# Recurrent branch of a four-mixer network: head outputs on the two halves of PSUM, products with the identity taken out, gate and bonus in the transposed layout

## The chip, the cores and the metric

The kernel runs on one core of a Trainium2 chip. The metric is the device time of one execution in microseconds. Three runs of the kernel before gave 2129.01, 2131.92 and 2132.62 us; the median is 2131.92 us. One further execution was recorded by the hardware profiler; it is the one whose rows are read below.

## The reference, cut to what matters

A network of two layers works on 512 tokens of width 1024, all in float32. Each layer projects the tokens, runs four mixers side by side (a windowed attention, a recurrent branch, an attention with forget gates, an attention over the 256 or fewer best keys), merges their gated outputs, and ends in a feed-forward part (dense in layer 0, eight experts in layer 1). The change touches the recurrent branch alone, which has 4 heads of 64:

```python
def step(state, inp):
    r_t, w_t, k_t, v_t, kk_t, a_t = inp
    sa = jnp.einsum('bhvk,bhk->bhv', state, -kk_t)
    state = (state * w_t[:, :, None, :] + sa[..., None] * (kk_t * a_t)[:, :, None, :]
             + v_t[..., None] * k_t[:, :, None, :])
    return state, jnp.einsum('bhvk,bhk->bhv', state, r_t)
...
y = ((y - ym) * lax.rsqrt(yv + RWKV_GN_EPS)).reshape(B, S, RWKV_W) * gn_g + gn_b
bonus = (jnp.sum(r_h * k_h * r_k, axis=-1, keepdims=True) * v_h).reshape(B, S, RWKV_W)
return ((y + bonus) * g).astype(p.dtype)
```

## The kernel before, in words

**Large products.** Projections, merge and feed-forward split each float32 operand into a high and a low part and run three products (L111, L112, L113) of 128 by 128 weights with 512 moving columns. ScalarE makes the high part of a weight block (L98), VectorE the low part (L99).

**The recurrent branch** (`rwkv`, L761 to L970) works on 8 chunks of 64 tokens. The 4 heads are two groups `g` of two heads `par`; a group's two heads lie on partitions 0 to 63 and 64 to 127 of a tile. A plain float32 product is two instructions in the trace, so four products show as x8; a transposition by `nc.tensor.transpose` shows as one. The stages:

- *Preparation* (`rwkv_prep`, L650 to L719), once for each group: normalised keys, two products with `wa_up` for decay and rate (L678, L683), the scaled keys `KBt` and queries `ARt`, and the bonus factor, four products with two columns each (L716).
- For each half of the sequence (`c0` = 0 and 4, four chunks):
  - *Pair matrices* `AM` (L819): for each pair of chunks and each head four products of 64 rows by 128 columns; then transpositions (L829, L830).
  - *Inversion* of the 64 by 64 triangles: 16 by 16 blocks by way of DRAM (`invert16`), then two levels of products (L848).
  - *Gap products* (L875, L885, L886): for each chunk the matrices `G` and `AP`, with a copy `xak` by ScalarE (L879) in the middle and another (L891) at the end.
  - *Rounds*, one for each chunk: `sa` = G + AP S, where G is brought in by a product with the identity (L901) and four small products are added (L906); `VS` written from it (L909 on VectorE, L910 on ScalarE); the output `y`, for each head a product with the state (L917) and one with `VS` (L919), all on the half of PSUM that the chunk has; the next state `u` = S + K'V, again with an identity product (L923) and four small ones (L928), then scaled by VectorE (L933) and copied by ScalarE (L937).
  - After two rounds the *normalisation* of 128 tokens (L941 to L967): statistics, scale and offset, bonus, gate product (L961), two transpositions (L965), and the split into high and low part (`put_o`, L512 to L514).

**Order.** The program is traced once and a planner of the framework lays down every engine's order beforehand from priorities and estimated durations; on the chip each engine then works its list in that order, waiting where a semaphore is not yet set. The recurrent branch has the highest priority (`hot`), and the work around it (value projection, the three attentions, gates and merge) is put where the branch waits. The branch's output is merged last of the four (`merge`). PSUM has eight banks; tags `r` and `y` are one bank each, so every stage of the branch passes through one or two banks. SBUF tiles with the tag `rw` come from a pool of 26.

Of the kernel before, what the change touches and what calls it, by code (L numbers as in the profile page):

```python
# [9 lines left out]
F32 = mybir.dt.float32  # L10
# [8 lines left out]
P = 128  # L19
# [17 lines left out]
TAGS = dict(rw=26, qk=14, o=12, pt=7, v=4, x=8, lc=4)  # L37
# [19 lines left out]
class Net:  # L57
# [219 lines left out]
    def load_vecs(self, layer):  # L277
# [5 lines left out]
        for name, src in (("mu", I["rwkv_mu"][layer]), ("w0", I["rwkv_w0"][layer]), ("a0", I["rwkv_a0"][layer]),  # L283
                          ("k_k", I["rwkv_k_k"][layer]), ("k_a", I["rwkv_k_a"][layer]),
                          ("r_k", I["rwkv_r_k"][layer].rearrange("h d -> (h d)")),
                          ("gb", I["gate_bias"][layer].rearrange("i d -> (i d)"))):
# [18 lines left out]
        self.gn = self.vec.tile([P, 2, 256], F32, name="gn", tag="gn")  # L305
        nc.sync.dma_start(self.gn[:, 0], I["rwkv_gn_g"][layer:layer + 1, :].to_broadcast([P, 256]))
        nc.sync.dma_start(self.gn[:, 1], I["rwkv_gn_b"][layer:layer + 1, :].to_broadcast([P, 256]))
# [342 lines left out]
    def rwkv_prep(self, g, r, k, wa, th, bonus):  # L650
# [26 lines left out]
        ps = self.ps("r")  # L677
        nc.tensor.matmul(ps, self.wa_up[0:64, gs], th[0:64], start=True, stop=True)  # L678
# [3 lines left out]
        ps = self.ps("r")  # L682
        nc.tensor.matmul(ps, self.wa_up[64:128, gs], wa[64:128], start=True, stop=True)  # L683
        a = self.bt("rw")
        nc.scalar.activation(a, ps, AF.Tanh, scale=0.5, bias=self.vcol("a0", g, True))
# [19 lines left out]
        for q in range(2):  # L705
            for par in range(2):
# [7 lines left out]
        bps = self.ps("r")  # L714
        for tb in range(TB):
            nc.tensor.matmul(bps[:, tb * 2:tb * 2 + 2], r[:, tb * P:(tb + 1) * P], self.halves[:, 0:P:64], start=True,  # L716
                             stop=True)
        nc.vector.tensor_copy(bonus[:, :, g], bps[:, 0:8].rearrange("p (t e) -> p t e", t=TB))
        return kb, ar, pc  # L719
# [40 lines left out]
    def rwkv(self, layer, pr):  # L760
        nc, bp = self.nc, self.bp  # L761
        r, k, v, wa, gl = pr[0:2], pr[2:4], pr[4:6], pr[6], pr[7]
        r4 = "p (c a t) -> p c a t"
        bonus = bp.tile([P, TB, 2, 2], F32, name="bonus", tag="bonus")
        nc.scalar.activation(wa[0:64], wa[0:64], AF.Tanh)
        KBt, ARt, pc = [], [], []
        for g in range(2):
            kb, ar, p_ = self.rwkv_prep(g, r[g], k[g], wa, wa, bonus)
# [6 lines left out]
        vt = [self.bt("rw").rearrange("p (t c) -> p t c", t=2) for _ in range(2)]  # L775
# [9 lines left out]

        for tb in range(TB):
# [4 lines left out]
            nc.scalar.copy(vt[tb // 2][:, tb % 2], ps[:, 0:256])  # L791
            p4 = ps[:, 0:256].rearrange("p (g e d) -> p g e d", g=2, e=2)
            for half in range(2):
                src = slice(64 * half, 64 * half + 64)
                ch = 2 * tb + half
                nc.vector.tensor_copy(VS(0, ch)[64:128], p4[src, :, 0])
                nc.vector.tensor_copy(VS(1, ch)[0:64], p4[src, :, 1])
        S = bp.tile([P, 2, 64], F32, name="S", tag="S", bufs=2)
        nc.vector.memset(S, 0.0)
# [3 lines left out]
        SD = SDs[0]  # L803
        ho = [self.new_o(("rwkv", g), "rw") for g in range(2)]
        idb = self.ident64[:, None].to_broadcast([P, 8, 64])
        for c0 in (0, 4):
# [4 lines left out]
            for c1 in (c0, c0 + 2):  # L811
                am = []
                for par in range(2):
                    rows = slice(64 * par, 64 * par + 64)
                    ps = self.ps("r")
                    for j in range(2):
                        for g in range(2):
                            i = 2 * j + g
                            nc.tensor.matmul(ps[:, i * P:(i + 1) * P], KB_(g, c1 + j)[rows], AR_(g, c1 + j)[rows],  # L819
                                             start=True, stop=True)  # L820
                    a = self.bt("rw").rearrange("p (i t) -> p i t", i=4)
                    nc.vector.tensor_mul(a, ps.rearrange("p (i t) -> p i t", i=4),
# [19 lines left out]
            def each(fn):  # L842
                ps = self.ps("r")
                for i in range(8):
                    for par in range(2):
                        rows = slice(64 * par, 64 * par + 64)
                        a, b2 = fn(c0 + i // 2, i % 2, par, i, rows)
                        nc.tensor.matmul(ps[rows, i * 64:(i + 1) * 64], a, b2, start=True, stop=True)  # L848
                return ps.rearrange("p (i t) -> p i t", i=8)

            def lower(ch, g, par):
                return am_(ch, g, par)[64 * par:64 * par + 64, 64 * par:64 * par + 64]
# [4 lines left out]
            self.invert16(c0 // 4, AM, tt, tT)  # L857
            for l in range(4, 6):
# [10 lines left out]
            for ch in range(c0, c0 + 4):  # L869
                ps = self.ps("r")  # L870
                for g in range(2):
                    for par in range(2):
                        rows = slice(64 * par, 64 * par + 64)
                        orow = slice(64 - 64 * par, 128 - 64 * par)
                        nc.tensor.matmul(ps[rows, g * 64:(g + 1) * 64],  # L875
                                         am_(ch, g, par)[orow, 64 * par:64 * par + 64], VS(par, ch)[orow, g],
                                         start=True, stop=True)
                x = bp.tile([P, 2, 64], F32, name="xak", tag="xak", bufs=2)
                nc.scalar.copy(x, ps[:, 0:128].rearrange("p (g t) -> p g t", g=2))  # L879
# [973 lines left out]
```

## Time and profile before

| what | us |
|---|---|
| median of three runs | 2131.92 |
| the profiled execution, its own time | 2129.68 |
| its span in the trace | 2127.9 |
| TensorE (PE) busy | 2040.7 |
| PE weight loads (PEld) busy | 1590.5 |
| VectorE (DVE) busy | 1365.3 |
| ScalarE (ACT) busy | 918.8 |
| GpSimd (POOL) busy | 150.3 |

The recurrent branch runs from about 60 to 333 us in layer 0 and from about 1020 to 1302 us in layer 1, mixed with other work. The busy time of PE counts each product from its start to its modelled end, and the ends of consecutive products overlap; how much PE time a product takes is read from the distance between its start and the start of the next. In the timeline, instructions of one line that follow each other stand in one row with a count; the first column is the start, the second the length.

### The profile page before, as it was taken

The page shows a single profiled execution, that of the slowest core. Times are in us where ns is not written, and L with a number is a line of the kernel's source. Part 1 is how long each engine was busy: PE and PEld are TensorE (multiplying, and loading weights), DVE is VectorE, ACT ScalarE, POOL GpSimd, SP SyncE. Part 2 cuts the span into 40 slices and gives each one's busy share as a digit, 9 for nine tenths or more (in the row PEclk, how much of TensorE's full clock was granted, in tenths as well). Part 3 has the DMA queues.
Part 4 walks back from the last instruction along what each step waited for, and adds up shares of the span by engine and source line. Part 5 has one row for each costly group of instructions (what it writes and reads, how often), then busy time and mean ns, then how long its engine had stood idle before and what let it go on. Part 6 is the DMA issues. An engine that isn't in the chain of part 4 may idle for free. (4 is left out here: it accounts for less than half of the span.)

```text
span 2127.9 us, 31168 instructions
## 1 busy us (share of the span) xinstructions
PE 2040.7 (96%) x11252; PEld 1590.5 (75%) x11252; DVE 1365.3 (64%) x2732; ACT 918.8 (43%) x1579; POOL 150.3 (7%) x211
## 2 busy tenths in 40 slices
PE   8999999999999999999999989999989999999984
PEld 7777767778888888888777767778877666677663
DVE  5775779844563333235686768844569777788778
ACT  3454533333232222113454533332317666677663
POOL 1020200000000000000011110000000000000034
PEclk9999999999999999999999999999999999999997
DMA  5231213243343334234221112323438988898872
GB/s 169 69 75 44 54 36 87 80 124 99 100 153 93 95 99 134 93 96 122 67 67 43 47 43 70 90 70 99 145 131 330 334 294 308 295 338 304 292 278 77
DMA packets 275537, 295.08 MB, mean 139 GB/s; under 512 B 23909, under 2 KB 203977, under 8 KB 275369
## 3 DMA queue, kind: packets, MB, share of 16 engines
q1 hardware_dynamic: 268296, 274.42, 40.4%
q0 software_dynamic: 7072, 18.49, 2.7%
q8 instruction: 97, 1.59, 0.3%
q14 instruction: 72, 0.58, 0.1%
HBM read 277.26 MB, written 15.60 MB: 138 GB/s over the span
## 5 line engine op out<-in xcount | busy, mean ns | idle before, releaser
L99 DVE TENSOR_TENSOR wlo<-wraw,whi 128x1024 fp32r<-128x1024 f32 (+1 forms) x218 | 265.4, 1218 | 373.4 <-ACT whi L98 370.4
L111 PE MATMUL ps_mm<-xh,whi 128*128 128x512 f32 (+1 forms) x1288 | 494.3, 384 | 3.2 <-ACT gate L977 2.6
L113 PE MATMUL ps_mm<-xh,wlo 128*128 128x512 f32 (+1 forms) x1288 | 494.3, 384 | 3.1 <-DVE rs L259 3.1
L98 ACT CAST whi<-wraw 128x1024 fp32r<-128x1024 f32 (+1 forms) x218 | 228.0, 1046 | 621.1 <-PE ps_mm L112 380.0
L112 PE MATMUL ps_mm<-xl,whi 128*128 128x512 f32 (+1 forms) x1288 | 495.1, 385 | 0.3 <-DVE xl L233 0.3
L111 PEld LDWEIGHTS ps_mm<-xh,whi 128*128 128x128 f32 x1288 | 243.9, 190 | 49.3 <-ACT gate L977 3.1
L113 PEld LDWEIGHTS ps_mm<-xh,wlo 128*128 128x128 f32 x1288 | 244.0, 190 | 47.4 <-DVE wlo L99 3.4
L112 PEld LDWEIGHTS ps_mm<-xl,whi 128*128 128x128 f32 x1288 | 244.0, 189 | 47.4 <-issue 4.8
L1152 DVE TENSOR_TENSOR wlo<-mwraw,whi 128x1024 fp32r<-128x1024 f32 (+1 forms) x98 | 124.1, 1281 | 18.9 <-ACT whi L1151 17.5
L1151 ACT CAST whi<-mwraw 128x1024 fp32r<-128x1024 f32 (+1 forms) x98 | 95.9, 1005 | 14.1 <-PE ps_t L1502 9.5
L472 ACT COPY bt_pt<-ps_t 128x512 f32<-128x512 f32 (+2 forms) x80 | 41.8, 522 | 100.2 <-PE ps_t L469 99.7
L1152 DVE TENSOR_TENSOR mwlo<-mwraw,mwhi 128x1024 fp32r<-128x1024 f32 (+1 forms) x62 | 71.8, 1174 | 7.0 <-ACT mwhi L1151 6.5
L453 ACT ACTIVATE bt_pt<-ps_s,mx 128x256 f32<-128x256 f32 (+3 forms) x128 | 62.0, 488 | 16.8 <-DVE mx L447 14.2
L444 DVE TENSOR_REDUCE mx<-ps_s 128x2 f32<-128x512 f32 (+3 forms) x80 | 48.5, 606 | 22.7 <-PE ps_s L408 22.0
L260 POOL TENSOR_TENSOR rs<-rs,mhalf 128x1 f32<-128x1 f32 x16 | 13.8, 861 | 693.7 <-DVE rs L259 693.7
L1151 ACT CAST mwhi<-mwraw 128x1024 fp32r<-128x1024 f32 (+1 forms) x62 | 61.0, 999 | 3.5 <-DMA mwraw<-in_exp_w_dram 2.3
L1113 DVE TENSOR_TENSOR bt_pt<-bt_pt,ps_mm 128x512 f32<-128x512 f32 x22 | 15.1, 687 | 70.5 <-PE ps_mm L113 63.1
L611 DVE MAX8 m<-bt_pt 128x8 f32<-128x256 f32 (+2 forms) x96 | 53.6, 558 | 2.2
L469 PE MATMUL ps_t<-ident,bt_pt 128*128 128x128 f32 x272 | 50.8, 282 | 4.2 <-DVE bt_pt L463 3.2
L1152 DVE TENSOR_TENSOR wlo<-ring,whi 128x1024 fp32r<-128x1024 f32 (+1 forms) x45 | 51.4, 1159 | 2.5 <-ACT whi L1151 1.5
L612 DVE MATCH_REPLACE8 bt_pt<-m,bt_pt 128x256 f32<-128x256 f32 (+2 forms) x96 | 52.0, 542 | 0.0
L111 PE MATMUL ps_mm<-bt_o,whi 128*128 128x512 f32 x128 | 51.2, 400 | 0.4 <-ACT gate L977 0.4
(709 smaller groups left out, 4172.0 us busy)
## 6 DMA issues: line engine op xcount, KB each, us to landing
mwraw<-in_exp_w_dram SPq DMA_DIRECT2D x124, 512.0 KB, 6.7
wraw<-in_w_in_dram SPq DMA_DIRECT2D x106, 512.0 KB, 3.7
wraw<-in_ffn_w_dram SPq DMA_DIRECT2D x66, 512.0 KB, 3.7
ring<-in_exp_w_dram SPq DMA_DIRECT2D x60, 512.0 KB, 6.0
wraw<-in_exp_w_dram SPq DMA_DIRECT2D x32, 512.0 KB, 6.0
mwraw<-in_exp_w_dram SPq DMA_DIRECT2D x36, 384.0 KB, 5.6
wraw<-in_w_branch_dram SPq DMA_DIRECT2D x20, 512.0 KB, 3.6
wraw<-in_w_out_dram SPq DMA_DIRECT2D x16, 512.0 KB, 3.7
```

The costliest lines, as they stand in the source:

```text
L98: nc.scalar.copy(h, src)
L99: (low or nc.vector).tensor_sub(l, src, h.bitcast(F32))
L111: mm(ps, wh, xh, start=start, stop=False)
L112: mm(ps, wh, xl, start=False, stop=False)
L113: mm(ps, wl, xh, start=False, stop=stop)
L444: nc.vector.tensor_reduce(mx[:, 0:nh], s3, op=OP.max, axis=AX.X)
L453: nc.scalar.activation(p3[:, h], s3[:, h], AF.Exp, bias=nm[:, h:h + 1], scale=0.125, accum_out=mx[:, 4 + h:5 + h])
L469: nc.tensor.transpose(pt[:, i * P:(i + 1) * P], p3[:, h, kb * P:(kb + 1) * P], self.ident)
L611: nc.vector.max(m8, sc[:, :nk])
L612: nc.vector.match_replace(sc[:, :nk], m8, sc[:, :nk], REPL)
L1151: self.chain("hi", lambda: nc.scalar.copy(hi[:, :n], src))
L1152: self.chain("lo", lambda: nc.vector.tensor_sub(lo[:, :n], src, hi[:, :n].bitcast(F32)))
```

## The change

What it does, stage by stage:

- The two `wa_up` products are issued one after the other into two banks (`r` and `y`).
- The bonus factor is one product with `halves` for all 512 tokens, at 128 by 512, and multiplied into `v`. Gate and offset are prepared once for each group in the layout with channels on partitions (`rwkv_gate`, after the first inversion), with the norm's scale and offset as per-partition columns. The broadcast copies `gn` go.
- The `AM` products of the two heads alternate, into the banks `r` and `y`.
- The gap products are made for two chunks at a time.
- In a round the identity products go: `G` is added by VectorE while `VS` is written, the old state is scaled ahead into `Sp` and added when the new state is read out of PSUM. The first round leaves out the products with the zero state.
- The outputs of a group's two heads go to the two halves of PSUM (chunk and group side by side), and are held behind the products of the next state by `issue_after`.
- After the normalisation eight products with a 64 by 64 identity bring the output into the transposed layout; it is multiplied by the gate and the prepared offset is added there.
- The pool `rw` has 28 tiles in place of 26, the scratch for dynamic DMA 4096 in place of 8192.

```diff
-        ps = self.ps("r")
-        nc.tensor.matmul(ps, self.wa_up[0:64, gs], th[0:64], start=True, stop=True)
+        ps, pa = self.ps("r"), self.ps("y")
+        nc.tensor.matmul(ps, self.wa_up[0:64, gs], wa[0:64], start=True, stop=True)
+        nc.tensor.matmul(pa, self.wa_up[64:128, gs], wa[64:128], start=True, stop=True)
...
+    def rwkv_gate(self, g, r, v, gl):
+        nc = self.nc
+        ps = self.ps("r")
+        nc.tensor.matmul(ps, self.halves, r, start=True, stop=True)
+        nc.vector.tensor_mul(v, v, ps)
+        ps = self.ps("r")
+        nc.tensor.matmul(ps, self.g_up[:, g * P:(g + 1) * P], gl, start=True, stop=True)
+        nc.scalar.activation(r, ps, AF.Copy, scale=self.vcol("gn_g", g))
+        nc.vector.scalar_tensor_tensor(v, v, self.vcol("gn_b", g), ps, op0=OP.add, op1=OP.mult)
+        return r, v
...
-                nc.vector.tensor_copy(VS(1, ch)[0:64], p4[src, :, 1])
+                nc.scalar.copy(VS(1, ch)[0:64], p4[src, :, 1])
...
+                pss = self.ps("r"), self.ps("y")
+                for j in range(2):
+                    for g, par in pairs:
+                        i = 2 * j + g
+                        rows = rows_[par]
+                        mm(pss[par][:, i * P:(i + 1) * P], KB_(g, c1 + j)[rows], AR_(g, c1 + j)[rows], start=True,
+                           stop=True)
...
-                    sa = self.ps("r")
-                    nc.tensor.matmul(sa[:, 0:128], self.ident, G[ch - c0].rearrange("p g t -> p (g t)"), start=True,
-                                     stop=True)
...
-                    nc.vector.tensor_copy(VS(0, ch)[0:64], s3[0:64])
-                    nc.scalar.copy(VS(1, ch)[64:128], s3[64:128])
+                        nc.vector.tensor_add(VS(0, ch)[0:64], s3[0:64], Gc[0:64])
+                        nc.vector.tensor_add(VS(1, ch)[64:128], s3[64:128], Gc[64:128])
...
+                            first = mm(u[rows_[par], g * 64:(g + 1) * 64], KT(ch)[:, g, rows_[par]], VS(par, ch)[:, g],
+                                       start=True, stop=True)
...
+                                nc.vector.scalar_tensor_tensor(Sn[:, g], us, d, Sp[:, g], op0=OP.mult, op1=OP.add)
...
+                            st.enter_context(self.tc.issue_after(first.ins))
                         for g in range(2):
+                            for par in (1, 0):
+                                o = yps[rows_[1 - par], half, g]
+                                if ch:
+                                    mm(o, ARt[g][ch // 4][:, ch % 4, 1 - par], SD[:, g, par], start=True, stop=False,
+                                       skip_group_check=True)
+                                mm(o, am_(ch, g, par)[:, rows_[1 - par]], VS(par, ch)[:, g], start=not ch, stop=True,
+                                   skip_group_check=True)
...
+                                nc.vector.tensor_scalar(Sp[:, g], S[:, g], pc[g][:, ch + 1:ch + 2], None, op0=OP.mult)
...
+                for half in range(2):
+                    for g, par in pairs:
+                        o = g * P + half * 64
+                        src = rows_[1 - par]
+                        mm(ps[rows_[par], o:o + 64], y[src, 2 * half + g], self.ident64[src], start=True, stop=True)
                 for g in range(2):
-                    self.put_o(ho[g], ts, ps[:, g * P:(g + 1) * P])
+                    gg, gb = go[g]
+                    t = bp.tile([P, P], F32, name="yt", tag="yt", bufs=2)
+                    nc.vector.tensor_mul(t, ps[:, g * P:(g + 1) * P], gg[:, ts])
+                    nc.vector.tensor_add(t, t, gb[:, ts])
+                    self.put_o(ho[g], ts, t)
```

## Rows read from the trace of the kernel before

**Rows 1.** The page, busy time, share of span, instructions.
```profile
PE 2040.7 (96%) x11252; PEld 1590.5 (75%) x11252; DVE 1365.3 (64%) x2732; ACT 918.8 (43%) x1579; POOL 150.3 (7%) x211
```

**Rows 2.** Windows: length, busy PE, PEld, DVE, ACT, POOL, granted clock, DMA share, GB/s.
```profile
60.00:333.00 273.00, 264.68 (x1947) 198.40 (x1946) 194.20 (x598) 132.38 (x338) 33.49 (x51) 0.99 0.22 55
1020.00:1302.00 282.00, 270.65 (x1965) 202.24 (x1965) 204.30 (x619) 135.09 (x340) 33.41 (x50) 0.99 0.20 52
```

**Rows 3.** Timeline of PE, large products back to back (start, length, line, tiles, form).
```profile
203.18 0.40 PE L111 MATMUL ps_mm<-xh,whi 128*128 128x512 f32 x1
203.41 0.39 PE L112 MATMUL ps_mm<-xl,whi 128*128 128x512 f32 x1
```

**Rows 4.** Timeline of PE, one round of the recurrence.
```profile
207.85 0.46 PE L901 MATMUL ps_r<-bt_rw,ident 128*128 128x128 f32 x2
208.23 0.45 PE L906 MATMUL ps_r<-S,bt_rw 64*64 64x64 f32 x8
208.61 0.50 PE L113 MATMUL ps_mm<-xh,wlo 128*128 128x512 f32 x1
208.95 0.40 PE L111 MATMUL ps_mm<-xh,whi 128*128 128x512 f32 x1
...
209.66 0.28 PE L917 MATMUL ps_y<-SD,bt_rw 128*64 128x64 f32 x2
209.78 0.28 PE L919 MATMUL ps_y<-bt_rw 128*64 128x64 f32 x2
...
210.46 0.49 PE L923 MATMUL ps_r<-S,ident 128*128 128x128 f32 x2
210.87 0.45 PE L928 MATMUL ps_r<-bt_rw 128*64 128x64 f32 x8
211.26 0.33 PE L469 MATMUL ps_t<-ident,bt_pt 128*128 128x128 f32 x1
```

**Rows 5.** Timeline of PE, gap products of one chunk.
```profile
180.03 0.45 PE L875 MATMUL ps_r<-bt_rw 64*64 64x64 f32 x8
180.41 0.33 PE L407 MATMUL ps_s<-bt_qk 128*128 128x128 f32 x1
...
180.91 0.34 PE L885 MATMUL ps_r<-xak,bt_rw 64*64 64x64 f32 x4
...
181.57 0.44 PE L469 MATMUL ps_t<-ident,bt_pt 128*128 128x128 f32 x2
```

**Rows 6.** Timeline of PE, pair matrices of one head and two chunks.
```profile
226.22 0.40 PE L111 MATMUL ps_mm<-xh,whi 128*128 128x512 f32 x1
226.54 1.16 PE L819 MATMUL ps_r<-bt_rw 64*128 64x128 f32 x8
227.63 0.39 PE L524 MATMUL ps_s<-m_swa,identb 128*128 128x512 bf16 x1
```

**Rows 7.** Timeline of PE, the first product with wa_up.
```profile
67.43 1.12 PE L678 MATMUL ps_r<-bt_rw,wa_up 64*128 64x512 f32 x2
68.48 0.48 PE L429 MATMUL ps_t<-whi,xh 128*128 128x456 f32 x1
```

**Rows 8.** Timeline of PE, the transposition of one finished block.
```profile
205.57 0.38 PE L965 MATMUL ps_r<-ident,ygn 128*128 128x128 f32 x2
205.71 0.48 PE L113 MATMUL ps_mm<-xh,wlo 128*128 128x512 f32 x1
```

**Rows 9.** Timeline of PE, gap products with nothing between them; brackets: idle before.
```profile
1253.88 0.45 PE L875 MATMUL ps_r<-bt_rw 64*64 64x64 f32 x8 [0.46 <-ACT bt_rw L891]
...
1255.88 0.45 PE L875 MATMUL ps_r<-bt_rw 64*64 64x64 f32 x8 [0.46 <-ACT bt_rw L891]
```

**Rows 10.** Window after that stretch, columns as in the second group.
```profile
1260.00:1265.00 5.00, 4.54 (x30) 3.17 (x28) 3.21 (x7) 0.96 (x3) 0.00 (x0) 0.50 0.02 5
```

**Rows 11.** Groups by line and form: count, busy us, mean ns, idle before.
```profile
L933 DVE TENSOR_SCALAR S<-ps_r,pc 128x64 f32<-128x64 f32 x28 | 6.7, 279 | 13.5 <-PE ps_r L928 13.5
L716 PE MATMUL ps_r<-halves,bt_rw 128*128 128x2 f32 x32 | 4.0, 248 | 0.4 <-DVE bt_rw L713 0.3
```

More of the change, by code (lines that the diff above doesn't have):

```diff
@@ L784, in AR_ @@
             return ARt[g][ch // 4][:, ch % 4].rearrange("p a t -> p (a t)")
+        rows_ = [slice(64 * par, 64 * par + 64) for par in range(2)]
+        pairs = [(g, par) for g in range(2) for par in range(2)]
         for tb in range(TB):
@@ L857, in rwkv @@
             self.invert16(c0 // 4, AM, tt, tT)
+            if c0 == 0:
+                go = [self.rwkv_gate(g, r[g], v[g], gl) for g in range(2)]
             for l in range(4, 6):
@@ new lines, in rwkv @@
+                for j in range(2):
+                    ch = c1 + j
+                    for g, par in pairs:
+                        o = j * P + g * 64
+                        mm(ps[rows_[par], o:o + 64], am_(ch, g, par)[rows_[1 - par], rows_[par]],
+                           VS(par, ch)[rows_[1 - par], g], start=True, stop=True)
+                x = bp.tile([P, 2, 2, 64], F32, name="xak", tag="xak", bufs=1)
+                nc.scalar.copy(x, ps[:, 0:256].rearrange("p (c g t) -> p c g t", c=2, g=2))
@@ new lines, in rwkv @@
+                ps = self.ps("r")
+                for j in range(2):
+                    ch = c1 + j
+                    for g, par in pairs:
+                        i, o, rows = (ch - c0) * 2 + g, j * 256 + g * 64, rows_[par]
+                        mm(ps[rows, o:o + 64], tT[rows, i], x[rows, j, g], start=True, stop=True)
+                        mm(ps[rows, o + 128:o + 192], AT[rows, ch - c0, g], tT[rows, i], start=True, stop=True)
+                gat = self.bt("rw").rearrange("p (c g t) -> p c g t", c=2, g=4)
@@ new lines, in rwkv @@
+                    SD, Gc = SDs[ch % 2], G[ch - c0]
+                    if ch:
+                        sa = self.ps("r")
+                        for g, par in pairs:
+                            rows = rows_[par]
+                            mm(sa[rows, g * 64:(g + 1) * 64], AP[ch - c0][rows, g], S[rows, g], start=True, stop=True)
+                        s3 = sa[:, 0:128].rearrange("p (g t) -> p g t", g=2)
+                        nc.vector.tensor_add(VS(0, ch)[0:64], s3[0:64], Gc[0:64])
+                        nc.vector.tensor_add(VS(1, ch)[64:128], s3[64:128], Gc[64:128])
+                    else:
+                        nc.vector.tensor_copy(VS(0, ch)[0:64], Gc[0:64])
+                        nc.scalar.copy(VS(1, ch)[64:128], Gc[64:128])
@@ L921, in rwkv @@
+                    first = None
                     if ch < NCH - 1:
                         u = self.ps("r")
-                        nc.tensor.matmul(u[:, 0:128], self.ident, S.rearrange("p g t -> p (g t)"), start=True,
-                                         stop=True)
+                        for g, par in pairs:
+                            first = mm(u[rows_[par], g * 64:(g + 1) * 64], KT(ch)[:, g, rows_[par]], VS(par, ch)[:, g],
+                                       start=True, stop=True)
+                        Sn = bp.tile([P, 2, 64], F32, name="S", tag="S", bufs=2)
@@ new lines, in rwkv @@
+                    if ch < NCH - 1:
+                        S, SD = Sn, SDs[(ch + 1) % 2]
+                        for par in range(2):
+                            nc.scalar.copy(SD[rows_[par], :, par], S[rows_[par]])
+                        if ch < NCH - 2:
+                            Sp = bp.tile([P, 2, 64], F32, name="Sp", tag="Sp", bufs=2)
+                            for g in range(2):
+                                nc.vector.tensor_scalar(Sp[:, g], S[:, g], pc[g][:, ch + 1:ch + 2], None, op0=OP.mult)
```

127 lines of the change are left out of this document (27 added, 100 removed).

## The prediction

> **What bounds the kernel now.** I read the page first: TensorE is busy for 2040.7 of 2127.9 us, VectorE for 1365.3 [rows 1]. Busy time alone doesn't make an engine the limit, because the modelled ends of products overlap. So the second view is the timeline of PE, where distances from start to start count: a large product starts 0.23 us after the one before it although it is shown 0.40 us long [rows 3]. The third view is the table by stage for the two stretches in which the recurrent branch lives, 60 to 333 and 1020 to 1302 us: PE busy for 264.7 of 273 and 270.7 of 282 us, VectorE for 194.2 and 204.3 [rows 2]. The branch's many waits are filled with projections and attention, so PE's list is nearly without holes there. The reader is to see that the branch's length is not what counts (its output is merged last). What counts is how much PE time its instructions take away from the large products. A microsecond of PE time saved in the branch should be a microsecond of the whole.
>
> **Three prices, from rows.** (1) *Pace*. Full-width products of 64 columns on one half of PSUM follow each other at 0.06 us: two of L917 start 0.12 us before the next two [rows 4]. Products that alternate between the two halves go faster: 8 of L875 take 0.38 us and 16 of L885 and L886 take 0.66 us, so 8 more cost 0.28, which is 0.035 each [rows 5]. (2) *Round trip*. Leaving full-size products for small ones and coming back costs about 0.30 us: 0.09 on entry (0.32 in place of 0.23 before L819) [rows 6], 0.10 on leaving (what is left of the 0.38 after 8 times 0.035) [rows 5], and 0.11 for the first large product afterwards (0.34 in place of 0.23) [rows 4]. (3) *128 columns*: 8 of L819, all of one head, take 1.09 us, so (1.09 - 0.10) / 8 = 0.124 each [rows 6].
>
> **The change part by part**, over both layers.
>
> *Rounds* (16). Before: L901 with L906 0.76, plus 0.11 after it; a pair of L917 issued alone, 0.30 + 2 x 0.06 = 0.42 (the run in the rows begins with L919); the other 14 output instructions 0.09 + 14 x 0.06 = 0.93; the switch to the identity product L923 0.09, itself 0.41, L928 0.39, and 0.11 after [rows 4]. Sum 3.21 us. After: the small products of `sa` alone, 0.30 + 8 x 0.035 = 0.58. Then `u` and the outputs in one run, as `issue_after` puts them: 0.30 + 8 x 0.035, and 16 output instructions. Those come four to a half, so three follow at 0.06 and the fourth is overlapped by the next half's first, about 0.01: 0.047 on average, 0.75. Sum 1.91, saving 1.30 in each of 12 middle rounds, 15.6 us. The two first rounds lose `sa` and half of the outputs: 0.30 + 16 x 0.035 = 0.86, saving 2.35 each, 4.7. The two last have no new state: before 3.21 - 0.09 - 0.41 - 0.39 = 2.32, after 0.58 + 0.30 + 0.75 = 1.63, saving 1.4 together. Total 21.7 us. Bounds for the outputs: no overlap (0.06 each, 14 x 0.21 = 2.9 less) and full alternation (0.035, 2.7 more).
>
> The row for products with 128 rows on alternating halves is L928: 8 in 0.39 us with 0.10 for leaving, 0.036 each, against 0.06 on one half [rows 4]. The Trainium skill (TensorE: Matmul & The Clock Gate, section on packing small matmuls) says that a weight load overlaps running products only where the row group differs, which would leave these outputs at 0.06 and the gain 2.9 us smaller; L928 doesn't bear it out, so I stay with the row.
>
> *Gap products* (8 pairs of chunks). Before, for each chunk (0.30 + 0.28) + (0.30 + 0.56) = 1.44; after, for two chunks 0.60 + 48 x 0.035 = 2.28 in place of 2.88 [rows 5]. Saving 0.60 x 8 = 4.8 us.
>
> *Pair matrices* (8 pairs of chunks). Before two runs of 0.09 + 1.09 + 0.11 = 1.29 [rows 6]. After, one run of 16 with the heads, and so the 64-row halves and the banks, alternating. The trace shows no such alternation with all 128 output columns. Bounds: no overlap, 0.30 + 16 x 0.124 = 2.28, saving 0.30 x 8 = 2.4; overlap as in rows 5, 0.30 + 16 x 0.062 = 1.29, saving 10.3. I take 10.3, since the alternating products of rows 5 differ in both halves and cost half, and these differ in rows and bank.
>
> *`wa_up`* (4 pairs). Before two runs of 0.09 + 1.05 + 0.11 = 1.25 [rows 7]; after, if the planner leaves them together, the last of one and the first of the other overlap: 0.30 + 3 x 0.48 = 1.74. Saving 0.76 x 4 = 3.0, between 0 and 3.0.
>
> *Last step* (8 blocks). Before 0.14 us without a change of form [rows 8]. After, 16 instructions of 64 by 64: 0.30 + 16 x 0.035 = 0.86. This costs 0.72 x 8 = 5.8 us more, 9.0 if they don't overlap (0.06 each). The Trainium skill (TensorEngine Tiling (Array Packing), section on PSUM pressure) says that different row tiles can't write one bank at the same time, which would give the 9.0; L875 alternates its row halves within one bank at 0.035 [rows 5], so the trace speaks for 5.8.
>
> *Bonus and gate.* L716 goes (4.0 us) [rows 11]; eight instructions of 512 columns come. The nearest row is L678, two of 512 columns in 1.05 [rows 7], so at most 4.2: I take 0, from 0 to -0.3. The gate product has the same columns in fewer pieces: 0.
>
> *Off PE, costed at nothing.* VectorE loses the per-head bonus (32 instructions), three 256-column passes for each of 8 blocks, and 32 copies that write `VS`; it gets two additions a round, the `Sp` scaling (24), two passes of 128 columns for each of 16 half blocks, and eight of 512 columns. An instruction of 64 columns takes 0.28 us [rows 11]. By count I get a balance near zero, within 10 us either way, and VectorE stands idle for 79 + 78 us in these stretches [rows 2]. Without that cover, 10 us would show in full. ScalarE is idle for over half of the time. SP issues two broadcast loads fewer and two small ones more in `load_vecs`; POOL's transfers for the inversion stay, and a smaller scratch would delay only them, and that wait is filled with large products as the others are. The bank `y` now also takes pair matrices and a `wa_up` product, so those wait until the outputs of the half before are copied out; they did not start earlier before. The two tiles of `rw` more make up for `r` and `v`, which are now kept to the end.
>
> *Waits added.* The outputs stand behind `u`, and `u` behind two additions on VectorE; behind `u` in PE's list stand the outputs and the filling products. The stall that goes (the copy on ScalarE after that on VectorE) is replaced by the second addition, 0.28 us [rows 11]: no difference.
>
> *Sum*: 21.7 + 4.8 + 10.3 + 3.0 - 5.8 = 34.0 us. From the profiled execution's own 2129.7 (2127.9 in the trace, 1.8 around it) that is 2095.7. The median of the runs is 2.2 above that execution, so 2098 for the median.
>
> **Rivals.**
>
> *The halves overlap less* (only what rows 4 and 5 show): pair matrices 2.4, `wa_up` 0, outputs and last step at 0.06: 34.0 - 7.9 - 3.0 - 2.9 - 3.2 = 17 us, 2115. For it: no row shows 64-row halves alternating with 128 columns out. Against it: L928 and L875.
>
> *VectorE takes over.* It is 71% and 72% busy in the two stretches [rows 2]; shortened by 17 us each, 76%, and unevenly so. If the large products then wait for their split weights, half of the gain is lost: 2115. Against it: 62 us idle are left in each.
>
> *More than the sum.* In layer 1 four chunks of gap products ran with nothing between them: 2.00 us a chunk in place of 1.44, PE waiting 0.46 us for one copy [rows 9], and the granted clock then stood at 0.50 for 5 us, the lower level of 1.2 GHz, after PE's waits [rows 10]. Halving the number of copies, and such a stretch not recurring, would give 4 x 0.56 + 2.5, and in both layers twice that: 9 us more, 2089.
>
> *Slower: the rounds run uncovered.* If the planner puts no large products between `sa` and `u` and between `u` and the next `sa`, PE waits for two VectorE instructions each time. One ScalarE copy cost 0.46 [rows 9]; two in turn some 0.9, so 1.8 a round, 29 us over 16 rounds; with four stretches at the lower clock, 2.5 us each [rows 10], 39, and the gap products uncovered as well 8 x 0.9 = 7 more: 2098 + 46 = 2144. It decides from 34 / 16 = 2.1 us of new waiting a round. Against it: in rows 4 filling products stand in both places.
>
> **How the numbers follow.** Forecast (2092 to 2108) 0.57; less overlap 0.14; VectorE 0.12; more 0.10; slower 0.07, of which 0.02 ends within 0.2% (4 us, about what a measurement of this kernel can tell from no change). The range 2085 to 2117 holds the first four and leaves the slower one and half of the edges out. Faster 0.92, same 0.03, slower 0.05.
>
> **What would show it.** Right: in the timeline no row of identity products in a round; `u` and outputs in one run of about 1.0 us; 16 pair-matrix instructions in about 1.1 us to the next start; gap products as x16 and then 32 in 0.66 and 1.2 us; the stages after each layer's merge unchanged in length, only earlier. Wrong: 16 pair-matrix instructions in 2.0 us (no overlap), runs of the branch with idle time in brackets and a granted clock under 1 in several windows (uncovered waits), or large products waiting for `wlo` (VectorE).

## The result, and the profile after

The changed kernel takes 2112.32 us (median of 4 runs, 2107.6 to 2114.26) against 2132.04 for the kernel before: a ratio of 0.9907, 95% interval 0.9888 to 0.9927. The profiled execution took 2107.6 us, its span went from 2127.9 to 2105.9. By the medians the change gave 19.7 us, between the two profiled executions 22.0, where I had forecast 34. The forecast of 2098 was 14 too low; the range held the time.

First the busy times and the two stretches of the branch, as in [rows 1, 2].

```profile
PE 2019.7 (96%) x11240; PEld 1569.9 (75%) x11240; DVE 1366.6 (65%) x2732; ACT 918.0 (44%) x1561; POOL 151.1 (7%) x211
```

```profile
60.00:333.00 273.00, 263.74 (x1992) 198.39 (x1991) 202.18 (x606) 134.67 (x333) 34.16 (x51) 1.00 0.23 60
1020.00:1302.00 282.00, 274.38 (x2034) 206.05 (x2034) 209.14 (x625) 139.78 (x337) 31.68 (x49) 1.00 0.22 58
```

In these two stretches PE is as full as before, and VectorE has the same total over the whole execution (1365.3 before). What each stage costs is read from start to start. One round, which answers to [rows 4]:

```profile
190.28 0.45 PE L902 MATMUL ps_r<-S,bt_rw 64*64 64x64 f32 x8
190.66 0.51 PE L111 MATMUL ps_mm<-xh,whi 128*128 128x512 f32 x1
...
192.73 0.45 PE L913 MATMUL ps_r<-bt_rw 128*64 128x64 f32 x8
193.01 0.34 PE L930 MATMUL ps_y<-SD,bt_rw 128*64 128x64 f32 x4
193.13 0.33 PE L932 MATMUL ps_y<-bt_rw 128*64 128x64 f32 x4
193.24 0.33 PE L930 MATMUL ps_y<-SD,bt_rw 128*64 128x64 f32 x4
193.36 0.34 PE L932 MATMUL ps_y<-bt_rw 128*64 128x64 f32 x4
193.62 0.49 PE L113 MATMUL ps_mm<-xh,wlo 128*128 128x512 f32 x1
```

There are no identity products, and state products and outputs stand in one run of 0.89 us. The planner also let the outputs of the two halves alternate one by one: 24 instructions in 0.89 - 0.10 us are 0.033 each. The gap products, for two chunks at a time (L877; L886 and L887 are before's L885 and L886), answer to [rows 5]:

```profile
173.26 0.68 PE L877 MATMUL ps_r<-bt_rw 64*64 64x64 f32 x16
173.88 0.45 PE L406 MATMUL ps_s<-bt_qk 128*128 128x384 f32 x1
...
174.58 0.34 PE L886 MATMUL ps_r<-xak,bt_rw 64*64 64x64 f32 x4
...
175.71 0.50 PE L113 MATMUL ps_mm<-xh,wlo 128*128 128x512 f32 x1
```

The two runs take 0.62 and 1.13 us, near the 0.66 and 1.2 that I had named. Next come the two edits that brought nothing, pair matrices (L817) and `wa_up` (L676, L677), against [rows 6, 7]:

```profile
197.99 1.16 PE L817 MATMUL ps_y<-bt_rw 64*128 64x128 f32 x8 [0.35 <-ACT ygn L945]
...
199.08 0.33 PE L406 MATMUL ps_s<-bt_qk 128*128 128x128 f32 x1
...
203.11 1.16 PE L817 MATMUL ps_r<-bt_rw 64*128 64x128 f32 x8
204.20 0.50 PE L112 MATMUL ps_mm<-xl,whi 128*128 128x512 f32 x1
```

```profile
32.50 1.12 PE L677 MATMUL ps_y<-bt_rw,wa_up 64*128 64x512 f32 x2
33.55 0.50 PE L113 MATMUL ps_mm<-xh,wlo 128*128 128x512 f32 x1
...
68.55 1.12 PE L676 MATMUL ps_r<-bt_rw,wa_up 64*128 64x512 f32 x2
69.60 0.47 PE L427 MATMUL ps_t<-whi,xh 128*128 128x456 f32 x1
```

The heads don't alternate at all: here the eight instructions into bank `y` stand 5 us ahead of the eight into bank `r`, each run 1.09 us long as before, and in none of the eight pairs of chunks do the banks alternate. The planner had parted what the code interleaves: in the rows shown, bank `r` was still taken by the last step (L962), while bank `y` had just been copied out (L945). The `wa_up` product into `y` went 36 us ahead of its partner. Last, the final step, against [rows 8]:

```profile
187.68 0.69 PE L962 MATMUL ps_r<-ident,ygn 64*64 64x64 f32 x12 [0.88 <-DVE ygn L955]
188.29 0.33 PE L405 MATMUL ps_s<-bt_qk 128*128 128x128 f32 x1
188.55 0.33 PE L962 MATMUL ps_r<-ident,ygn 64*64 64x64 f32 x4
```

PE stands still for 0.88 us until the normalised output is there, and the run is broken in two, so it pays the round trip twice. All eight blocks are broken in two.

Summed over both layers (each instruction from its start to the next start, and the excess of the large product before a run added to the run):

| PE time, us | before | after | saved | forecast |
|---|---|---|---|---|
| rounds | 50.4 | 22.3 | 28.1 | 21.7 |
| gap products | 27.2 | 15.8 | 11.4 | 4.8 |
| pair matrices | 20.5 | 21.2 | -0.7 | 10.3 |
| `wa_up` | 9.1 | 9.1 | 0.0 | 3.0 |
| last step | 3.0 | 15.1 | -12.1 | -5.8 |
| bonus and gate | 8.4 | 5.8 | 2.6 | 0 |
| other stages of the branch | 50.0 | 52.2 | -2.2 | 0 |
| whole branch | 168.6 | 141.5 | 27.1 | 34.0 |

So the branch gave back 27.1 us, and 22 arrived. Landmarks in the timeline say where the other 5 went: the first product of layer 0's output projection (L1034 before, L1035 after) came 10.3 us earlier, its feed-forward part then took 2.4 us longer (553.6 to 967.0 before, 543.3 to 959.1 after), layer 1 gained 12.8 more up to its output projection, and the rest 1.3. Up to the two output projections 23.1 of the 27.1 us had arrived; 4 went to waits outside the branch. These are in layer 1: about 10 of the 27 us were saved in layer 0, where all of it arrived, and 17 in layer 1. The window around the end of layer 1's last attention, before and after, and PE's longest wait there after the change:

```profile
1390.00:1420.00 30.00, 30.00 (x158) 23.37 (x158) 14.07 (x23) 11.29 (x20) 0.00 (x0) 1.00 0.25 71
1390.00:1420.00 30.00, 26.20 (x130) 20.64 (x129) 10.27 (x17) 8.22 (x15) 0.00 (x0) 0.89 0.18 53
PE ps_t L467 <- DVE bt_pt L461: 2.8, 1, 2.8
```

Before, PE was busy throughout at the full clock; now it waits for the softmax of that attention, and the granted clock stands at 0.50 from 1395 to 1400 us. In layer 0 the trace shows no wait of PE between 400 and 460 us.

### The profile page after: what moved, and what is told of

Read it like the earlier page. It is cut to its first block, busy times and chain, and to the rows that moved or that the text cites. A ratio compares the mean times of both kernels' runs of the same rounds, so it can differ in the third digit from the quotient of the medians.

```text
span 2105.9 us, 31148 instructions
## 1 busy us (share of the span) xinstructions
PE 2019.7 (96%) x11240; PEld 1569.9 (75%) x11240; DVE 1366.6 (65%) x2732; ACT 918.0 (44%) x1561; POOL 151.1 (7%) x211
## 5 line engine op out<-in xcount | busy, mean ns | idle before, releaser
L1114 DVE TENSOR_TENSOR bt_pt<-bt_pt,ps_mm 128x512 f32<-128x512 f32 x22 | 15.1, 688 | 70.4 <-PE ps_mm L113 63.0
L467 PE MATMUL ps_t<-ident,bt_pt 128*128 128x128 f32 x272 | 51.5, 283 | 6.0 <-DVE bt_pt L461 4.8
```

Source lines behind the costliest of these rows:

```text
L467: nc.tensor.transpose(pt[:, i * P:(i + 1) * P], p3[:, h, kb * P:(kb + 1) * P], self.ident)
```

## The experiments

All were timed in turn with the kernel before, and the ratio is to the kernel before of the same rounds. *Branch on PE* is the total of the table above for that kernel's profile; *search ends* gives the start of the last instruction of VectorE's search for the best keys, which the last (sparse) attention waits for, in layer 0 and in layer 1; *distance* is from the last product of that attention to the first of the output projection, in both layers.

| kernel | median us | ratio [95%] | branch on PE | search ends | distance |
|---|---|---|---|---|---|
| before | 2132.04 | 1 | 168.6 | 399.9, 1355.8 | 109.3, 118.8 |
| after | 2112.32 | 0.9907 [0.9888, 0.9927] | 141.5 | 396.7, 1354.4 | 100.6, 100.9 |
| e1 | 2109.96 | 0.9894 [0.9879, 0.9908] | 139.5 | 395.6, 1355.0 | 101.7, 101.6 |
| e2 | 2105.2 | 0.9874 [0.986, 0.9888] | 137.8 | 398.4, 1351.5 | 99.9, 99.8 |
| e3 | 2102.85 | 0.9865 [0.9851, 0.9879] | 133.0 | 393.2, 1346.0 | 100.5, 100.9 |
| e4 | 2114.05 | 0.9911 [0.9898, 0.9925] | 150.7 | 388.2, 1355.5 | 114.3, 106.0 |
| e5 | 2108.16 | 0.9884 [0.9869, 0.99] | 141.2 | 397.2, 1355.8 | 100.6, 101.7 |
| e6 | 2107.75 | 0.9884 [0.9868, 0.99] | 146.5 | 394.2, 1353.5 | 106.0, 100.5 |
| e7 | 2115.46 | 0.9916 [0.9902, 0.993] | 137.3 | 399.5, 1359.8 | 100.8, 101.7 |
| e8 | 2121.47 | 0.9932 [0.9917, 0.9947] | 137.9 | 404.8, 1367.3 | 101.7, 101.8 |
| e9 | 2109.38 | 0.989 [0.9873, 0.9908] | 146.4 | 403.5, 1361.2 | 100.5, 95.1 |
| e10 | 2097.68 | 0.9829 [0.9814, 0.9844] | 139.3 | 404.9, 1355.8 | 87.5, 87.5 |
| e11 | 2133.44 | 1.0005 [0.9996, 1.0014] | 170.7 | 402.3, 1361.4 | 109.3, 118.9 |
| e12 | 2093.95 | 0.9815 [0.9801, 0.9828] | 138.6 | 402.7, 1351.4 | 87.3, 87.3 |

**e1: heads forced to alternate** (and the two `wa_up` products in the same way).

```diff
...
+                        with ExitStack() as st:
+                            if last is not None:
+                                st.enter_context(self.tc.issue_after(last.ins))
+                            last = mm(pss[par][:, i * P:(i + 1) * P], KB_(g, c1 + j)[rows], AR_(g, c1 + j)[rows],
+                                      start=True, stop=True)
...
```

> The changed kernel, but the pair-matrix products of the two heads are held in the order in which they are written (head 0, head 1, head 0, ...), and so are the two wa_up products of a group; in the changed kernel's trace the planner had parted them by bank (8 of L817 into ps_y, later 8 into ps_r, 1.09 us each, as before the change). Theory A (the forecast's 10.3 and 3.0 us failed to come because the order never alternated, not because the engine can't): 16 instructions in 1.1 to 1.3 us to the next start in place of two runs of 1.09 with a round trip each, the second wa_up product overlapped by about half a microsecond; 10 to 13 us of PE time less, time 2100 to 2104. Rival B (64-row halves with all 128 output columns do not overlap): 16 instructions in about 2.0 us, only round trips are saved, 2.4 us, time 2108 to 2112.

The timeline of PE in e1, the pair matrices (L822):

```profile
114.58 0.37 PE L822 MATMUL ps_r<-bt_rw 64*128 64x128 f32 x1
114.58 0.37 PE L822 MATMUL ps_y<-bt_rw 64*128 64x128 f32 x1
...
115.47 0.27 PE L822 MATMUL ps_y<-bt_rw 64*128 64x128 f32 x1
115.67 0.49 PE L548 MATMUL ps_s<-tri,bt_pt 128*128 128x128 f32 x2
```

Sixteen take 1.09 us, as long as eight of one head: the overlap that I had taken is real. Five of the eight pairs take this long; two others are followed by a wait, and one takes 2.01 us at a granted clock of 0.50. Pair matrices fell from 21.2 to 12.7 us and `wa_up` from 9.1 to 6.8. So theory A is right on the engine and wrong on the time: that fell by 2.4 us, within the spread of the runs, and the branch as a whole by 2.0. Waits ahead of other runs took the place (the first product of the key norms 0.8 us in the changed kernel and 3.3 in e1, the transpositions of `v` 1.7 and 3.7, those of `KBt` 2.2 and 4.5, the last step 8.0 and 9.1), and PE's waits for the softmax of the attentions (L467 for L461) rose from 4.8 to 9.3 us. The granted clock up to the output projections was 0.99 and 0.98 on average, against 1.00 and 0.99.

**e2: outputs on the chunk's half, two transpositions at the end.**

```diff
...
-                                o = yps[rows_[1 - par], half, g]
+                                o = yps[rows_[half], 2 * g + par]
...
-                        mm(ps[rows_[par], o:o + 64], y[src, 2 * half + g], self.ident64[src], start=True, stop=True)
+                    nc.tensor.transpose(ps[:, g * P:(g + 1) * P], y2[:, g * P:(g + 1) * P], self.ident)
...
```

> The changed kernel with one part undone: the outputs of a round go to the half of PSUM that belongs to the chunk, as before the change, and two 128 by 128 transpositions take the place of the eight 64 by 64 products at the end of a block. Theory A (outputs gain by alternating halves, the last step loses): outputs 16 at 0.06 us in place of about 0.03, +0.45 us in each of 14 rounds and +0.2 in the two first, 6.5 us in all; the last step loses the two runs of 12 and 4 with their round trips, about 1.0 us in each of 8 blocks, 8 us; so 2109 to 2113. If the wait of about 1 us before the last step, which the changed kernel shows, belongs to the form of these products, it goes too: 2102 to 2106. Rival B (the halves are worth most of the gain): 2118 to 2124.

The outputs cost 6.9 us more without the alternation (0.06 each again) and the last step 9.4 less (5.7 us), as theory A had it. So the two halves for the outputs save less than the small products at the end cost. The time fell further, by 7.1 us, into the range that I had tied to the wait's going; but the wait went only in part (2.6 us in 5 times, 4.3 in 6 in the changed kernel), so this part of the gain is not explained by it.

**e3: the last step behind the next round's state products.**

```diff
...
+                    with ExitStack() as st:
+                        if after is not None:
+                            st.enter_context(self.tc.issue_after(after.ins))
...
+                if tb == TB - 1:
+                    finish(None)
+                else:
+                    todo.append(finish)
...
```

> The changed kernel, but the eight products at the end of a block are issued behind the next round's state products (for the last block of the layer as before). Theory A (PE's list has these products too early, and PE stands still at them while GpSimd and VectorE finish the normalisation): 6 of 8 waits of 0.4 to 0.9 us go, and runs no longer break into 12 and 4; 4 to 7 us less, 2105 to 2109. Rival B (the wait moves to the next instruction that needs bank r, or the list is drawn otherwise and loses elsewhere): 2110 to 2115.

The time is 2102.9, 9.5 us below the changed kernel and below the range of theory A, whose direction it has. The last step fell from 15.1 to 9.4 us, its waits for the normalised output from 4.3 us in 6 times to 0.4 in one (1.8 us in 3 times now wait for the state). The step had cost 8.2 us beyond my price of 0.86 a block; two thirds of that were this wait and the broken runs.

**e4: identity products back in rounds 1 to 7.**

```diff
...
+                        mm(sa[:, 0:128], self.ident, Gc.rearrange("p g t -> p (g t)"), start=True, stop=True)
...
+                            mm(u[:, 0:128], self.ident, S.rearrange("p g t -> p (g t)"), start=True, stop=True)
...
```

> The changed kernel with one part undone: in rounds 1 to 7 G and the old state are brought in by products with the identity again, VS is written by VectorE and ScalarE, and Sp is gone. Theory A (PE time is what counts): 0.28 us more in sa and 0.50 in the new state (two 128-column instructions and a change of form each) in 14 and 12 rounds, about 10 us, time 2120 to 2124. Rival B (the identity products were hidden or their removal is paid for by the two additions in a row on VectorE): 2110 to 2115.

The branch costs 9.2 us more PE time, as theory A priced it, but the time is only 2 us longer than the changed kernel's, which is rival B's range: the identity products are hidden. **e5: the two memory settings of before** and **e6: gap products one chunk at a time** belong with it.

```diff
-TAGS = dict(rw=28, qk=14, o=12, pt=7, v=4, x=8, lc=4)
+TAGS = dict(rw=26, qk=14, o=12, pt=7, v=4, x=8, lc=4)
...
```

> The changed kernel with the two memory settings of before (26 tiles of rw in place of 28, DMA scratch of 8192 in place of 4096); the computation is the same. Theory A (the settings cost and give nothing, what is lost is lost in the branch's order): 2108 to 2116 us, and the branch's groups within 2 us of the changed kernel's. Rival B (the fewer tiles hold products back, so that part of the gain hangs on them): over 2118 us, with new waits of the branch for a tile of rw. Rival C (the smaller scratch delays transfers): under 2106 us, with the waits for DMA shorter. Whatever it is, the difference shows how far two orders of the same work stand apart.

```diff
-            for c1 in (c0, c0 + 2):
+            for c1 in range(c0, c0 + 4):
                 ps = self.ps("r")
-                for j in range(2):
+                for j in range(1):
...
```

> The changed kernel with the gap products one chunk at a time again, as before (16 runs of 8 and of 16 products in place of 8 runs of 16 and of 32, two copies a chunk). Theory A (price of the round trip, 0.30 us, twice a pair of chunks less): +4.8 us of PE time in these groups, 2115 to 2119 us. Rival B (what the change saved there was the uncovered stretch of layer 1): the groups cost 11 us more as before, idle time of 0.4 us ahead of several runs and a granted clock below 1 in that stretch, 2119 to 2126 us. Rival C (PE time given back is taken by waits elsewhere, so PE time added is hidden as well): 2110 to 2114 us.

e5 is theory A (2108, every stage within 1 us): the settings do nothing, and differences of some 4 us among these kernels are not to be read. e6 adds 5.0 us of PE time in the branch, as its theory A priced it, and its time is that of e5, below even the numbers of rival C: PE time added is hidden. No uncovered stretch came back, so the edit on the gap products is not what removed it. Together e1, e4 and e6 say that PE time in the branch, given or taken, no longer moves the end by itself. e2 and e3 are no exception: in both VectorE's search in layer 1 ended earlier (1351.5 and 1346.0 us, 1354.4 in the changed kernel), which the next runs show to be what counts.

**e7: e2 and e3 together; e8: with the alternation of e1 added.**

> The edits of e2 and of e3 together: outputs on the chunk's own half, two transposes of 128 columns at the end, and these issued behind the next round's state products. Theory A (both runs removed the same wait for the normalised output): not additive, 2100 to 2105 us; outputs 6 to 7 us dearer than in the changed kernel, last step about 3 us in place of 15. Rival B (e2 won by fewer small products, e3 by the wait, two things): -7 and -9 add up, 2094 to 2098 us.

> e7 with the heads of the pair matrices and of wa_up alternating as in e1. Theory A (the waits that ate e1's gain were those of products moved together with the branch's scarce banks and tiles, and stay): PE time of pair matrices and wa_up 10 to 11 us less than in e7, the time only 0 to 4 us less, 2097 to 2104 us. Rival B (what ate e1's gain was the last step, which stood in the way of the same bank y): the whole 10 us come through, 2090 to 2095 us.

Both theories missed, in e7 and in e8: they are slower than the changed kernel, with 4 us less PE time in the branch. The windows of e8 around the last attention of each layer, and PE's waits in 400 to 460:

```profile
400.00:430.00 30.00, 28.63 (x155) 21.24 (x154) 20.98 (x53) 13.04 (x37) 0.00 (x0) 1.00 0.30 84
430.00:460.00 30.00, 22.13 (x111) 16.33 (x110) 10.61 (x27) 9.23 (x22) 0.00 (x0) 0.77 0.39 114
1390.00:1420.00 30.00, 22.15 (x120) 16.07 (x121) 11.88 (x31) 10.28 (x25) 0.00 (x0) 0.77 0.07 18
```

```profile
PE ps_t L467 <- DVE bt_pt L461: 4.0, 2, 2.7
PE ps_s L624 <- ACT bt_pt L451: 2.7, 3, 1.4
PE ps_o L481 <- ACT bt_pt L470: 2.0, 3, 0.7
```

PE has run out of other work and stands at several steps of the last attention, and the granted clock falls to 0.77 on average. The last column of the table tells why: after that attention 100 to 102 us follow in e8, e7, e1, e2, e3, e5 and the changed kernel alike. They are the merge of the sparse attention and of the recurrent branch behind it: 16 gates of 24 products and 16 times 6 are 480, and less two gates made ahead 432, 98 us at 0.227. Counted in the traces, 432 products stand there in layer 1 of each of these kernels, and 432 or 437 in layer 0; in the kernel before there were 476 and 518. In none of them, with that order, was more of it moved forward, so a layer ends no sooner than the attention's end plus 100 us. The attention ends 44 to 48 us after the search in all kernels of the table, and the search is VectorE's. In these seven kernels the execution ends 750 to 756 us after the search of layer 1, while their profiled spans differ by 21 us. Here are the search in the changed kernel from 305 to 397 us, and all engines (columns as in [rows 2]) in its last 64 us:

```profile
L609 DVE MAX8 m<-bt_pt 128x8 f32<-128x256 f32 (+2 forms) x48 | 26.9, 560 | 1.3
L610 DVE MATCH_REPLACE8 bt_pt<-m,bt_pt 128x256 f32<-128x256 f32 (+2 forms) x48 | 26.1, 543 | 0.0
```

```profile
333.00:397.00 64.00, 64.00 (x283) 51.84 (x281) 62.21 (x124) 19.11 (x27) 0.00 (x0) 1.00 0.31 90
```

VectorE is busy for 62.2 of 64 us; of the 92 us from 305 to 397 the search takes 57 and the low parts of weights 19. Before the change 9 and 18 us of free products were left behind the attention (109.3 and 118.8 against 100). The change used them up. It did not bring the search forward as it did the other work: against the start of its layer the search ended 3.2 us earlier in layer 0 and 6.5 us later in layer 1 than before.

**e9 to e11: the recurrent branch merged ahead of the sparse attention**, in the changed kernel, in e8, and in the kernel before.

```diff
...
-        order = (("fox", 2, 2, 768), ("swa", 0, 4, 0), ("dsa", 3, 2, 1024), ("rwkv", 1, 2, 512))
+        order = (("fox", 2, 2, 768), ("swa", 0, 4, 0), ("rwkv", 1, 2, 512), ("dsa", 3, 2, 1024))
...
```

> The changed kernel with one edit outside the branch: in the merge, the recurrent branch (ready 100 to 150 us before the sparse attention) is merged ahead of the sparse attention and not behind it. In the changed kernel each layer's output projection begins 100.6 and 100.9 us after the last product of the sparse attention (109.3 and 118.8 us in the kernel before), and that attention ends 46 us after VectorE's search for the largest scores. Theory A (the layer's end now hangs on that search, since 100 us of merging that could fill PE stand behind it): with some 50 us of merging moved ahead of it, the waits ahead of the last attention's products go, 5 to 10 us less, 2102 to 2107 us, and the distance falls to 50 to 90 us. Rival B (PE's list is full there, and the missing 12 us are dearer products in the branch alone): 2109 to 2114 us.

> e8 with the merge order of e9. Theory A (e8 had the PE time of e7 or less in the branch and lost it all to waits of the last attention for VectorE's search, 13 and 10 us in the stretches 400 to 500 and 1400 to 1500 us): these waits go, and 2094 to 2102 us are left, 20 us or more below e8. Rival B (the waits belong to the search itself, whatever may fill them, or return elsewhere): 2112 to 2122 us.

> The kernel before with the merge order of e9, as a control. Theory A (before the change PE still had 9 and 18 us of merging left after the last attention, beyond the 100 us that wait for it, so the search set nothing): 2127 to 2134 us, no more than 5 us gained. Rival C (the order of the merge is worth the same in any kernel, and has nothing to do with the branch): as much below the kernel before as e9 is below the changed kernel.

e10 is theory A: 23.8 us below e8, with the same products. The windows of e10, with the columns of [rows 2]:

```profile
400.00:430.00 30.00, 28.61 (x155) 21.26 (x154) 21.16 (x53) 13.01 (x37) 0.00 (x0) 1.00 0.31 85
430.00:460.00 30.00, 29.90 (x171) 22.73 (x170) 15.49 (x33) 12.40 (x26) 0.00 (x0) 1.00 0.42 129
1390.00:1420.00 30.00, 30.00 (x158) 23.56 (x157) 13.30 (x24) 12.09 (x21) 0.00 (x0) 1.00 0.25 70
```

In layer 0 the search ended where it had in e8 (404.9 against 404.8), and PE worked through. e11 is theory A too: the same order is worth nothing in the kernel before. e9 is undecided: its 2109.4 lies in rival B's range, but its runs spread from 2103.7 to 2113.0, over both ranges, and the distance fell in layer 1 alone (95.1), not to the 50 to 90 of A. Layer 1 gained 18.7 us up to its output projection against 12.8 in the changed kernel, as A has it, but layer 0 lost 6.8 us to a fall of the clock that the changed kernel's profile doesn't show (below).

**e12: the working tiles moved by 128 bytes**, in e10.

```diff
...
+        pad = self.vec.tile([P, 32], F32, name="pad", tag="pad")
+        nc.vector.memset(pad, 0.0)
...
```

> e10 with an unused tile of 128 bytes a partition, set to zero, put ahead of the working tiles, which moves all of them by 128 bytes to the same position within a block of 2048 bytes as in the kernel before. In the kernel before the large products of the feed-forward part follow each other at 0.229 us, in every changed kernel at 0.233 to 0.234; the part lasts 413.4 us before (553.6 to 967.0) and 415.6 to 416.3 after, though nothing in it was changed. Theory A (the place of the tiles in memory sets this pace): 0.229 us again, 413.4 us, and 2 us less in all, 2093 to 2098 us. Rival B (something else, the place is indifferent): 0.233 us and 415.6 us, the time as in e10, 2095 to 2100 us. In both, the layer's ends as in e10.

Three products of the feed-forward part in the changed kernel and then in e12:

```profile
872.20 0.39 PE L1037 MATMUL ps_t<-whi,bt_qk 128*128 128x512 f32 x1
872.43 0.40 PE L1035 MATMUL ps_o<-whi,bt_qk 128*128 128x512 f32 x1
872.67 0.39 PE L1036 MATMUL ps_o<-wlo,bt_qk 128*128 128x512 f32 x1
872.90 0.40 PE L1037 MATMUL ps_o<-whi,bt_qk 128*128 128x512 f32 x1
```

```profile
872.29 0.39 PE L1053 MATMUL ps_s<-whi,bt_qk 128*128 128x512 f32 x1
872.51 0.39 PE L1051 MATMUL ps_t<-whi,bt_qk 128*128 128x512 f32 x1
872.74 0.39 PE L1052 MATMUL ps_t<-wlo,bt_qk 128*128 128x512 f32 x1
872.97 0.39 PE L1053 MATMUL ps_t<-whi,bt_qk 128*128 128x512 f32 x1
```

Three take 0.70 us and 0.68. The mean from 870 to 950 us is 0.2333 and 0.2297, in the kernel before 0.2289, and the part lasts 413.4 us again. This is theory A: 2.4 us of the change's gain went to the place of its tiles, through temporaries that were added and removed. It is the length of this part that shows it; the intervals of the whole times of e10 and e12 overlap. e12 has the lowest median of the study, 0.9815 [0.9801, 0.9828] of before.

## Why the prediction was right and wrong

**What bounds.** "A microsecond of PE time saved in the branch should be a microsecond of the whole" held only while free products were left behind the last attention, 9 and 18 us, and failed from there: in the changed kernel that is layer 1, where 4 us did not arrive. I had read VectorE's idle time in the stretches of the branch, and not the stretch after it, where VectorE has almost none. e8 and e10 show it: the same branch, 2121 or 2098 us by what may stand beside the search. The rival "VectorE takes over" named the engine, but another place and another wait (large products waiting for split weights; in the trace it is the last attention that waits, for the search and for its softmax).

**Rounds.** The mechanism was right in every row, and mis-sized low: 28.1 for 21.7. Outputs alternated one by one (0.033 for my 0.047), and those of the kernel before had cost 26.7 us over all rounds, where the one round of [rows 4] gave 16 times 1.35, 21.6. The Trainium skill (TensorE: Matmul & The Clock Gate, section on packing small matmuls) lets a weight load overlap running products only where the row group differs. The outputs above use all 128 rows and alternate between halves of columns alone, and they follow each other at 0.033 us against 0.06 on one half (e2), so the trace decides against it here.

**Gap products.** The round trips were priced right: undone in e6 they cost 5.0 us. The other 6.6 have two sources. Before, 16 chunks cost 27.2 where 1.44 each is 23.0; this is for the most part the uncovered stretch of [rows 9, 10], which I had put in a rival. After, a pair cost 1.97 where I had 2.28.

**Pair matrices and `wa_up`.** This is the step of the sum that failed: 13.3 us forecast, and -0.7 came. The price was right (16 in 1.09, e1). What failed was "if the planner leaves them together", a condition that I had named for `wa_up` alone: the planner parted the products for two banks, of which one came free earlier.

**Last step.** Mis-sized: 12.1 for 5.8. The 0.86 a block holds for an unbroken run that waits for nothing. I had named a wait for the rounds and none here, where the products wait for the end of the normalisation. e3 takes most of that wait away and two thirds of the excess with it.

**VectorE, gate, memory.** VectorE's total changed by 1.3 us, as counted; gate and bonus gave 2.6 us; the memory settings gave nothing (e5).

**The number.** Forecast were 34.0 us; the branch gave 27.1; 2.4 went to the tiles' place, 4 to waits outside the branch, and 1.3 came back behind, which makes 22. The rivals "halves overlap less" and "VectorE takes over" both end next to the measured time, at 2115; the cause of the first is refuted by e1, the second had the engine alone right. The misses of the two pair terms and the last step (-20.3) and the gains of rounds, gap products and gate (+15.6) partly cancelled, so it is in part luck that the range held.

What stays open: the planner's order differs in each of these kernels, and what sets the end of the search (8 us later in layer 0 of e8 than in the changed kernel, 8 us earlier in layer 1 of e3) was not tried apart.

## What to carry to other kernels

Before pricing PE time saved in one branch, ask what the layer's end waits for and how many products can still be put ahead of it: the distance from the last dependent result to the stage's end tells how much saving counts. An overlap that depends on the order of instructions is to be forced, and then read in the timeline, when a planner orders them. A layer's last merge should be the one whose input comes last; this was worth 23.8 us in e10 and nothing in e11, where free products were still left.

## What the runs showed of the hardware

*Same list, same waits, another clock.* Windows of four microseconds from 200 us, in e9 and then in the changed kernel:

```profile
200.00:204.00 4.00, 3.52 (x22) 2.34 (x23) 2.47 (x11) 0.56 (x3) 0.58 (x1) 0.69 0.00 0
204.00:208.00 4.00, 4.00 (x13) 2.61 (x11) 1.85 (x5) 1.53 (x7) 0.29 (x1) 0.50 0.00 0
208.00:212.00 4.00, 4.00 (x17) 3.30 (x17) 2.30 (x4) 2.44 (x7) 1.01 (x2) 0.50 0.45 89
```

```profile
200.00:204.00 4.00, 3.52 (x31) 2.40 (x29) 3.03 (x14) 1.38 (x6) 0.36 (x1) 1.00 0.00 0
204.00:208.00 4.00, 4.00 (x28) 3.27 (x27) 3.04 (x4) 3.33 (x10) 1.30 (x2) 1.00 0.21 39
208.00:212.00 4.00, 4.00 (x23) 3.02 (x23) 3.67 (x11) 0.93 (x5) 1.00 (x2) 1.00 0.48 131
```

Up to there PE's list is the same instruction by instruction. In both PE had waited 0.88, 0.35 and 0.48 us between 187 and 201 us, in the same order, 0.24 us apart. In e9 the granted clock then stood at 0.50 (1.2 GHz) until about 215 us, in the changed kernel it stayed at 1.00. The difference is 6.8 us, as much as the runs of one kernel are apart.

*Row halves.* Four `wa_up` instructions on the two halves of the rows take 1.06 us in e1 (68.10 to 69.16), two on one half 1.05.

*Place of the tiles.* 128 bytes changed the pace of products whose order and shape were the same throughout the feed-forward part, from 0.2333 us in the changed kernel and the same in e10 to 0.2297 in e12. This holds for about its last 110 us; ahead of these, from 80 to 280 us into the part, all three run at the same mean pace of 0.227 us. Which of the operands matters was not tried.
